# Attention's branch product as seven Strassen products, with its quadrant sums and the pooling's moving sums accumulated in DRAM

## The chip, the cores and the metric

The kernel runs on one core of one Trainium2 chip. The metric is the device time in microseconds of one execution; the median of three is given. A profile is one further execution, recorded instruction by instruction; its span runs from the first to the last recorded instruction.

## The reference

One decoder block on 1024 tokens of width 1024, all in float32. What matters here is its first half:

```python
h = _rmsnorm(x, g_mix_pre[l])
proj = jnp.einsum('bsd,de->bse', h, w_in[l]) + b_in[l]
u_pool, q, k, v, gates = jnp.split(proj, IN_SPLITS, axis=-1)
y_pool = _multiscale_pool(u_pool, w_pool[l], pool_scale[l])
...
y_attn = _sliding_window_sink_attention(...)
g = jax.nn.sigmoid(gates.astype(jnp.float32)).astype(x.dtype)
g_pool, g_attn = g[..., :D_MODEL], g[..., D_MODEL:]
merged = (g_pool * jnp.einsum('bsc,cd->bsd', y_pool, w_branch_pool[l])
          + g_attn * jnp.einsum('bsc,cd->bsd', y_attn, w_branch_attn[l]))
mix = jnp.einsum('bsd,de->bse', merged, w_out[l])
```

`_multiscale_pool` takes 512 channels in four groups of 128, and for each group subtracts the value itself from the mean over the last 2, 4, 8 or 16 tokens (fewer at the start). The attention has 8 query heads of 64, so the attention branch multiplies a 1024 x 512 by a 512 x 1024 matrix. After `mix` come a norm, a squared-ReLU MLP of width 4096 and another norm.

## The kernel before

Every matmul is float32 in three passes (`PASSES`): each operand is split into a rounded part `hi` (ScalarE, L101) and the rest `lo` (VectorE, L104), and hi x hi, hi x lo and lo x hi are added in PSUM. A matmul has 128 x 128 weights and 512 columns. Data is stored with features on the partitions and tokens along the free dimension.

The stages follow each other: q, k and v; attention, in whose gaps the pool projections `u` are made (`u_half`, stored to `u_dram`) and whose outputs are stored and accumulated in `y_dram`; the gates; the attention branch; the pool branch; the output product; the MLP.

The gates, a 1024 x 1024 by 1024 x 2048 product, are already seven Strassen products per pair p of column blocks (`Pairs`, p from 0 to 7): products 1 and 2 of all pairs first, then `rest(p)` with products 6, 7, 5, 4, 3, of 12 matmuls each. Operand sums are made by VectorE (L484 to L494), results close with a scale (L713, L717), a sigmoid on ScalarE and a store to `z_dram`.

The attention branch is `branch(w_ba[m], ...)` for m from 0 to 7: load the weights, split them, and multiply 4 k-tiles in three passes for both halves `th` of the tokens (`mm_fm`, L445 and L447) into two banks, which VectorE multiplies into the gate tiles `zg` (L932). Its right side is read by `load_attn` from `y_dram` during the last gate pair: four quadrants, each [128, 2, 512], split once. Between column blocks, `pool_part` loads a group's `u` and computes its pooled difference on VectorE (`pool_in`): log2(w) additions of a shifted copy (L692), each with a small copy of the edge (L693), then scale and subtract; a split follows. The pool branch then does the same as the attention branch with weights `wbp_dram` and right side `ysp`.

`wo_load` and `wo_add` make sums of quadrants of the output weights: SP loads a quadrant into SBUF, and a GpSimd transfer with `accum_op` adds the other (L966).

Order of work: in most of the first half the program order of PE, VectorE and ScalarE is written by hand (`manual_schedule`); in the gates' second pass and the branches a scheduler of the tile framework places each engine's instructions, SP's and GpSimd's included. Tiles come from pools with a fixed number of buffers: a load waits until the last reader of its buffer is done. DMA completions are counted on eight semaphores for SP and ScalarE together and eight for GpSimd, in turn, so that a transfer also waits for the one that used its semaphore before. SP, ScalarE and GpSimd start their instructions in order, so a wait holds up all that stands behind it.

## Time and profile before

| | |
|---|---|
| time, median of 3 (lowest to highest) | 1110.14 us (1108.49 to 1111.05) |
| the profiled execution | 1109.43 us |
| its span | 1107.6 us |
| instructions | 13855 |
| mean granted TensorE clock | 0.998 |
| DMA: moved, mean rate | 203.71 MB, 184 GB/s |

The profile page gives busy time per engine, slices of the span, the chain of work that ended last and the costliest groups. PE is TensorE's matmul stream, PEld its weight loads, DVE VectorE, ACT ScalarE, POOL GpSimd, SP the engine that issues most DMAs. A row such as `PE mm L445 <- ACT wh L101: 0.2, 1, 0.2` reads: PE's instruction of line 445 writing tile mm waited for ScalarE's of line 101 writing wh, 0.2 us in total, once, 0.2 us at the longest. In the timeline the columns are start, duration, engine, line, operation and tiles, and in brackets the idle time before it with who ended it.

### The profile page before, as it was taken

The page shows a single profiled execution, that of the slowest core. Times are in us where ns is not written, and L with a number is a line of the kernel's source. Part 1 is how long each engine was busy: PE and PEld are TensorE (multiplying, and loading weights), DVE is VectorE, ACT ScalarE, POOL GpSimd, SP SyncE. Part 2 cuts the span into 40 slices and gives each one's busy share as a digit, 9 for nine tenths or more (in the row PEclk, how much of TensorE's full clock was granted, in tenths as well). Part 3 has the DMA queues.
Part 4 walks back from the last instruction along what each step waited for, and adds up shares of the span by engine and source line. Part 5 has one row for each costly group of instructions (what it writes and reads, how often), then busy time and mean ns, then how long its engine had stood idle before and what let it go on. Part 6 is the DMA issues. An engine that isn't in the chain of part 4 may idle for free.

```text
span 1107.6 us, 13855 instructions
## 1 busy us (share of the span) xinstructions
PE 1097.7 (99%) x5108; PEld 907.5 (82%) x5108; DVE 807.1 (73%) x1175; ACT 547.6 (49%) x916; POOL 62.7 (6%) x107
## 2 busy tenths in 40 slices
PE   9999999999999999999999999999999999999997
PEld 7888788888888888878888888888888888888886
DVE  5578867899768796899878867666548944456596
ACT  7466656444432337587555654444434434344342
POOL 0344220000001120000000000000000000000000
PEclk9999999999999999999999999999999999999999
DMA  9406578355677581570457645445597535534673
GB/s 349 161 11 137 149 169 278 132 191 209 224 256 246 152 186 58 192 271 32 162 197 264 242 169 199 146 151 199 178 371 232 189 98 174 177 102 152 204 229 119
DMA packets 89747, 203.71 MB, mean 184 GB/s; under 512 B 8400, under 2 KB 21072, under 8 KB 89680
## 3 DMA queue, kind: packets, MB, share of 16 engines
q1 hardware_dynamic: 77536, 176.88, 48.0%
q10 hardware_dynamic: 5616, 19.66, 4.6%
q0 software_dynamic: 6528, 6.29, 4.0%
q8 instruction: 40, 0.66, 0.3%
q14 instruction: 27, 0.22, 0.1%
HBM read 147.23 MB, written 55.58 MB: 183 GB/s over the span
## 4 chain that ended last, share of the span: by engine, by line
PE 88%; DVE 5%; DMA 3%; ACT 2%; issue 2%; DVEq 0%; SPq 0%; ACTq 0%
PE mm L511 24%; PE at L511 16%; PE at L1406 16%; PE mm L1406 12%; PE mm L601 4%; PE mm L187 3%; PE mm L445 2%; PE at L196 1%; PE at L419 1%; PE mm L447 1%; PE sc L355 1%; PE sc L187 1%; DMA d<-spill_dram 1%; PE at L1048 1%; PE mm L1048 1%
## 5 line engine op out<-in xcount | busy, mean ns | idle before, releaser
L1406 PE MATMUL at<-ar,wh 128*128 128x512 f32 x744 | 169.6, 389 | 0.0
L1406 PEld LDWEIGHTS at<-ar,wh 128*128 128x128 f32 x744 | 139.6, 188 | 29.3 <-DVE ar L104 0.4
L104 DVE TENSOR_TENSOR wh<-raw,wh 128x1024 fp32r<-128x1024 f32 x53 | 64.8, 1223 | 99.4 <-ACT wh L101 99.4
L1406 PE MATMUL mm<-ar,wh 128*128 128x512 f32 x576 | 131.0, 389 | 0.0
L101 ACT CAST wh<-raw 128x1024 fp32r<-128x1024 f32 x53 | 55.8, 1053 | 146.7 <-PE at L1406 71.6
L1406 PEld LDWEIGHTS mm<-ar,wh 128*128 128x128 f32 x576 | 108.1, 188 | 22.4
L101 ACT CAST wh<-st 128x512 fp32r<-128x512 f32 (+1 forms) x97 | 61.6, 646 | 74.4 <-PE at L511 19.9
L104 DVE TENSOR_TENSOR wh<-st,wh 128x512 fp32r<-128x512 f32 (+1 forms) x97 | 68.8, 719 | 27.8 <-ACT wh L101 25.3
L511 PE MATMUL mm<-gr,wh 128*128 128x512 f32 x333 | 80.4, 391 | 0.0
L511 PEld LDWEIGHTS mm<-gr,wh 128*128 128x128 f32 x333 | 62.1, 188 | 13.1 <-DVE gr L1087 0.4
L511 PE MATMUL mm<-T,wx 128*128 128x512 f32 x288 | 67.6, 389 | 0.0
L511 PEld LDWEIGHTS mm<-T,wx 128*128 128x128 f32 x288 | 54.1, 188 | 11.2
L511 PE MATMUL at<-T,wx 128*128 128x512 f32 x252 | 59.1, 389 | 0.0
L511 PEld LDWEIGHTS at<-T,wx 128*128 128x128 f32 x252 | 47.3, 188 | 9.8
L511 PE MATMUL mm<-x,wh 128*128 128x512 f32 x240 | 55.2, 389 | 0.0
L511 PEld LDWEIGHTS mm<-x,wh 128*128 128x128 f32 x240 | 45.0, 188 | 9.4
L104 DVE TENSOR_TENSOR ar<-B,ar 128x1024 fp32r<-128x1024 f32 x37 | 45.1, 1219 | 4.0 <-ACT ar L101 3.9
L601 PE MATMUL mm<-x,wh 128*128 128x512 f32 x192 | 47.5, 395 | 0.0
L101 ACT CAST ar<-B 128x1024 fp32r<-128x1024 f32 x37 | 38.9, 1051 | 5.9 <-DMA B<-in_w_dn_dram 3.0
L601 PEld LDWEIGHTS mm<-x,wh 128*128 128x128 f32 x192 | 35.3, 188 | 7.7
L511 PE MATMUL at<-gr,wh 128*128 128x512 f32 x150 | 36.7, 390 | 0.0
L101 ACT CAST wx<-ws 128x512 fp32r<-128x512 f32 x30 | 18.6, 620 | 32.7 <-DVE ws L487 17.9
(384 smaller groups left out, 2162.4 us busy)
## 6 DMA issues: line engine op xcount, KB each, us to landing
raw<-f_dram SPq DMA_DIRECT2D x53, 512.0 KB, 3.7
f_dram<-g SPq DMA_DIRECT2D x30, 512.0 KB, 3.3
B<-in_w_dn_dram SPq DMA_DIRECT2D x24, 512.0 KB, 6.3
st<-in_w_up_dram SPq DMA_DIRECT2D x20, 512.0 KB, 4.1
st<-in_w_g_dram SPq DMA_DIRECT2D x18, 512.0 KB, 4.6
f_dram<-g ACTq DMA_DIRECT2D x17, 512.0 KB, 2.6
g<-spill_dram SPq DMA_DIRECT2D x16, 512.0 KB, 5.4
raw<-in_w_dn_dram SPq DMA_DIRECT2D x16, 512.0 KB, 4.7
```

The lines of the kernel that those rows point to most:

```text
L101: act.copy(hi, src)
L104: eng.tensor_tensor(lo, src, f32(hi), ALU.subtract)
L187: pe.matmul(bq, xs_[k][n // 4][:, xh, n % 4 * P:(n % 4 + 1) * P], wq[k][:, h, :], start=k == 0 and j == 0, stop=k == NK - 1 and j == 2)
L196: pe.matmul(bkv_of(n), xs_[k][n // 4][:, xh, n % 4 * P:(n % 4 + 1) * P], wkv[k // 2][:, h, k % 2, :], start=k == 0 and j == 0 and not (joi ...
L355: pe.matmul(sb[:, kv, i, :nk], qt[r, qx, m * P:(m + 1) * P], kx[r, k0:k0 + nk], start=j == 0, stop=j == 2)
L419: pe.matmul(flat(yb), v[:, kv, :], flat(p[:, 4 * kv:4 * kv + 4]), start=j == 0, stop=j == len(mms) - 1)
L445: pe.matmul(bs[th], whi[:, k, :], rhs(k, hl, th), start=k == 0 and hl == 0, stop=False)
L447: pe.matmul(bs[th], wlo[:, k, :], rhs(k, 0, th), start=False, stop=k == nk - 1)
L511: pe.matmul(b, w[:, wh, kt, :], xo[kt][:, xh, :], start=not after and kt == 0 and j == 0, stop=kt == 3 and j == 2, skip_group_check=after)
L601: pe.matmul(b, (whi, wlo)[h][:, k, :], xr(k, xh, th), start=j == 0, stop=j == len(mms) - 1)
L1048: pe.matmul(bs[t], gop[i][kt // 2][gh][:, kt % 2, t * P:(t + 1) * P], wop[i][kt // 2][wh][:, kt % 2], start=not after and kt == 0 and j == ...
L1406: pe.matmul(bs[t], fo[fh][:, k2, t * P:(t + 1) * P], wo_[wh][:, k2, :], start=not after and s2 == 0 and k2 == 0 and j == 0, stop=s2 == NS ...
```

## The change

The attention branch becomes seven products (`Halves`) on 2 x 2 quadrants: the weights of a pair of column blocks give A11, A12, A21, A22 and the sums S1 to S4, the attention output gives B11, B21, B22 and T1 to T4. For p from 0 to 3, `first(p)` does products 1 and 2, `rest(p)` products 5, 6, 3, 7, 4; each is 2 k-tiles x 3 passes = 6 matmuls of 512 columns. Product 6 is added onto product 1 in its bank, then 7, then 4; 3 is added onto 5. ScalarE copies the bank out after 1, 5 and 1+6, VectorE reads it after 2, 3, 7 and 4, and the next product into that bank comes after the read.

The sums T1 to T4 are made in DRAM (`quad_sums`, in the spill buffer): a quadrant is loaded, negated on ScalarE and stored by GpSimd, and further quadrants are added by accumulating transfers from DRAM to DRAM. T1 and T4 come out negated and are negated again when they are split. The moving sums are made in the same way (`window_sums`): `u` is stored twice, and for each step a GpSimd transfer adds the sum of the step before, shifted by 1, 2, 4 or 8 tokens; from the second step on it first copies it. `pool_in` then needs only a scale on ScalarE, the edge, and one subtraction.

The gates' second pass is written differently too: `side()` after each product makes one operand of the next pair and runs the new steps from a table `extra`, keyed by pair and step; SP's and GpSimd's orders are now as written (`manual_schedule`), and loads come two pairs ahead. The sum of output weights `sums` is loaded in pair 2 and added to in pair 3 of the branch, without the copy that tied it to a gate tile.

```diff
             nc.sync.dma_start(u_dram[gi], u)
+            nc.sync.dma_start(sum_dram[gi][0], u)
...
-        while step < w:
-            t = place()
-            dve.tensor_tensor(t[:, step:], src[:, step:], src[:, :S - step], ALU.add)
-            dve.tensor_copy(t[:, :step], src[:, :step])
-            src, step = t, 2 * step
...
+    def window_sums(step):
+        for gi in (1, 0, 2, 3):
+            if 1 << step < WINDOWS[gi]:
+                src, dst = (sum_dram[gi][step - 1] if step else u_dram[gi]), sum_dram[gi][step]
+                if step:
+                    pool.dma_start(dst, src, max_dma_last_dim=4096)
+                pool.dma_start(dst[:, 1 << step:], src[:, :S - (1 << step)], accum_op=ALU.add)
+    def pool_in(gi, u, t):
+        w, bias = WINDOWS[gi], vec[:, V_BU + gi:V_BU + gi + 1]
+        act.activation(u, u, AF.Identity, bias=bias)
+        edge = t[:, :w - 1]
+        dve.scalar_tensor_tensor(edge, edge, float(w), cst[:, C_CNT:C_CNT + w - 1], ALU.mult, ALU.mult)
+        act.activation(t, t, AF.Identity, bias=bias, scale=1.0 / w)
+        dve.tensor_tensor(u, t, u, ALU.subtract)
...
+    def quad_sums(part):
+        if part == 0:
+            negate(("T1", "T3"), 0, 1)
+            add("T3", y_dram[1][:, 2:4])
+            add("T1", y_dram[0][:, 0:2])
+        else:
+            negate(("T4",), 1, 0)
+            pool.dma_start(t_dram["T2"], t_dram["T3"], max_dma_last_dim=4096)
+            add("T2", y_dram[0][:, 0:2])
+            add("T4", t_dram["T2"])
...
+        PRODUCT = {1: ("A11", "B11"), 2: ("A12", "B21"), 3: ("S4", "B22"), 4: ("A22", "T4"),
+                   5: ("S1", "T1"), 6: ("S2", "T2"), 7: ("S3", "T3")}
...
+        def rest(self, p, sides, between):
+            z, x, t, t2 = zg[self.base, p], self.x.pop(p), self.tmp.pop(p), g32([2, 512])
+            y = self.bank(p)
+            self.mm(y, p, 5)
+            act.copy(t2[:, 0], y)
+            sides[0]()
+            self.mm(x, p, 6, True)
+            act.copy(t[:, 0], x)
+            sides[1]()
+            self.mm(y, p, 3, True)
+            dve.tensor_tensor(t[:, 0], t[:, 0], y, ALU.add)
+            dve.tensor_tensor(z[1][:, 0], z[1][:, 0], t[:, 0], ALU.mult)
+            sides[2]()
+            self.mm(x, p, 7, True)
+            dve.tensor_tensor(t2[:, 0], t2[:, 0], x, ALU.add)
+            dve.tensor_tensor(z[1][:, 1], z[1][:, 1], t2[:, 0], ALU.mult)
+            sides[3]()
+            between()
+            self.mm(x, p, 4, True)
+            dve.tensor_tensor(z[0][:, 1], z[0][:, 1], x, ALU.mult)
...
+        extra = {(0, 2): lambda: quad_sums(0), (1, 0): lambda: quad_sums(1), (1, 3): lambda: window_sums(1),
+                 (2, 3): lambda: window_sums(2), (3, 3): lambda: window_sums(3),
...
+                 (7, 3): lambda: (ba.load("T4"), ba.split("T3", gr))}
...
-    for m in range(8):
-        branch(w_ba[m], lambda k, hl, th: asp[th][k // 2][hl][:, k % 2, :], 8, m)
+        for p in range(4):
...
+            pool_load(p)
+            if p == 2:
+                sums = wo_load((1, 0), a32)
+            elif p == 3:
+                wo_add(sums, (1, 1))
+            ba.rest(p, (nothing if p < 0 else lambda: w_next(p), nothing, lambda: w_split(p),
+                        lambda: pool_split(p)),
+                    (lambda: ba.first(p + 2)) if p < 2 else nothing)
```

What this moves, in the order of the built programs. PE at the head of the attention branch, before (yahi and yalo are the split attention output, wh the split weights, mm_491 and mm_492 the banks of the two halves of the tokens):

```order
L445 MATMUL mm_491_3135<-yahi_475_3058,wh_489_3131 128x512
L445 MATMUL mm_491_3135<-yalo_476_3059,wh_489_3131 128x512
L445 MATMUL mm_492_3136<-yahi_478_3064,wh_489_3131 128x512
L445 MATMUL mm_492_3136<-yalo_479_3065,wh_489_3131 128x512
L447 MATMUL mm_491_3135<-yahi_475_3058,wh_490_3132 128x512
L447 MATMUL mm_492_3136<-yahi_478_3064,wh_490_3132 128x512
```

Each of the eight column blocks has four such rows of six, in two banks; neither bank is read before all four k-tiles are in. After, PE from the end of product 5 of pair 0 over its product 6 to its product 7 (at_510 is the bank of products 1, 6, 7 and 4 of pair 0, at_526 that of 5 and 3, at_534 that of product 1 of pair 2; gr and wo are split quadrants of the attention output, ar and wh split weights; a second run through the same three passes is left out):

```order
L983 MATMUL at_526_3266<-wo_496_3122,ar_451_2835 128x512
L983 MATMUL at_510_3207<-gr_504_3163,ar_450_2834 128x512
L983 MATMUL at_510_3207<-gr_505_3164,ar_450_2834 128x512
L983 MATMUL at_510_3207<-gr_504_3163,ar_451_2835 128x512
L983 MATMUL at_534_3318<-wo_470_2982,wh_528_3279 128x512
L983 MATMUL at_534_3318<-wo_471_2983,wh_528_3279 128x512
L983 MATMUL at_534_3318<-wo_470_2982,wh_529_3280 128x512
L983 MATMUL at_510_3207<-gr_507_3182,wh_448_2832 128x512
```

The bank at_510 holds product 1 already, so its product 6 stands behind the copy of line 994 out of it, and product 7 behind that of line 1007; between 6 and 7 stand four matmuls of another bank.

ScalarE in the branch after, with the semaphores that each instruction waits for (L994, L1004 and L1007 are the copies after product 1, product 5 and products 1+6; at_510 and mm_515 are the banks of pairs 0 and 1 for 1, 6, 7 and 4, at_526 and mm_542 those for 5 and 3; z_ is the last gate, d_ are the pooling's tiles, ar and wh take split weights):

```order
L994 COPY g_511_3208<-at_510_3207 128x512 [waits PE_49]
L719 DMA spill_dram<-z_472_2986 128x1024 [waits Activation_49]
L994 COPY g_516_3234<-mm_515_3233 128x512 [waits PE_49]
L1007 COPY g_511_3208<-at_510_3207 128x512 [waits DVE_49,PE_49]
L1004 COPY g_525_3265<-at_526_3266 128x512
L994 COPY g_535_3319<-at_534_3318 128x512 [waits PE_49]
L104 CAST ar_546_3367<-ws_543_3360 128x768 [waits DVE_49,PE_49]
L104 CAST wh_544_3365<-st_520_3255 128x1024 [waits DMAHW3_49,PE_49]
L704 ACTIVATE d_523_3261<-d_523_3261,vec_83 128x1024 [waits DMAHW6_49,DMAHW4_49]
L1004 COPY g_541_3351<-mm_542_3352 128x512 [waits DVE_49,PE_49]
L707 ACTIVATE d_524_3262<-d_524_3262,vec_83 128x1024 [waits DMAHW7_49,DVE_49]
L1007 COPY g_516_3234<-mm_515_3233 128x512 [waits PE_49,Activation_49]
```

Before, the same stretch of ScalarE held the last sigmoids, casts of weights, one bias per pooling group and the cast of its difference, and nothing that reads PSUM. Now the copies of pair 1 (L1004, L1007) stand behind two casts and the pooling's L704 and L707, of 768 and 1024 elements.

GpSimd after, from the first store of a negated quadrant to the first window sums (all names are pieces of the spill buffer in DRAM except neg, a negated quadrant in SBUF, and y_dram; DMASW are GpSimd's DMA semaphores):

```order
L859 DMA spill_dram<-neg_396_2403 128x1024 [waits DMASW4_49,Activation_49]
L859 DMA spill_dram<-neg_396_2403 128x1024 [waits DMASW5_49]
L862 DMA spill_dram<-y_dram 128x1024 [waits DMASW5_49,DMASW6_49,DMASW2_49,DMASW7_49,DMASW1_49,DMASW0_49]
L862 DMA spill_dram<-y_dram 128x1024 [waits DMASW4_49]
L859 DMA spill_dram<-neg_407_2476 128x1024 [waits Activation_49]
L871 DMA spill_dram<-spill_dram 128x1024 [waits DMASW6_49]
L862 DMA spill_dram<-y_dram 128x1024 [waits DMASW1_49]
L862 DMA spill_dram<-spill_dram 128x1024 [waits DMASW3_49,DMASW2_49,DMASW0_49]
L698 DMA spill_dram<-spill_dram 128x1024
L699 DMA spill_dram<-spill_dram 128x1022 [waits DMASW4_49]
L698 DMA spill_dram<-spill_dram 128x1024
L699 DMA spill_dram<-spill_dram 128x1022 [waits DMASW7_49,DMASW6_49]
```

Eight more rows of L698 and L699 follow, the last an addition of 1016 columns, and then the sums of the output weights (L1066). Before, these sums (L966) came next after the additions into y_dram; now twenty transfers stand ahead of them, and most of these wait for the landing of one just before.

214 lines of the change are left out of this document (156 added, 58 removed).

## The prediction

> **What bounds the kernel now.** I read the page first, its busy line and its chain of waits.
>
> ```profile
> span 1107.6 us, 13855 instructions
> PE 1097.7 (99%) x5108; PEld 907.5 (82%) x5108; DVE 807.1 (73%) x1175; ACT 547.6 (49%) x916; POOL 62.7 (6%) x107
> PE 88%; DVE 5%; DMA 3%; ACT 2%; issue 2%; DVEq 0%; SPq 0%; ACTq 0%
> ```
>
> TensorE is busy throughout and the chain that ends last is 88% TensorE. A busy PE need not be at its peak, so I next asked who PE waited for. These are all of its waits in the run:
>
> ```profile
> PE mm L205 <- DVE zeros L183: 1.5, 1, 1.5
> PE sc L355 <- DVE s L364: 0.8, 2, 0.5
> PE at L1094 <- DVE x L1063: 0.4, 1, 0.4
> PE mm L445 <- ACT wh L101: 0.2, 1, 0.2
> ```
>
> Under 3 us of 1107.6. Then the stages around the change, by windows (columns: PE, PEld, DVE, ACT, POOL busy; granted clock; DMA share; GB/s): the second pass over the gates, the attention branch, the pool branch, the start of the output product.
>
> ```profile
> 209.70:318.90 109.20, 109.17 (x482) 89.94 (x481) 91.49 (x137) 49.17 (x67) 0.00 (x0) 1.00 0.62 210
> 318.90:362.40 43.50, 43.50 (x193) 36.03 (x192) 35.19 (x57) 12.63 (x15) 4.16 (x4) 1.00 0.79 251
> 362.40:406.00 43.60, 43.45 (x192) 35.55 (x191) 37.09 (x44) 15.12 (x18) 10.06 (x9) 1.00 0.67 173
> 406.00:440.00 34.00, 34.00 (x152) 28.15 (x151) 23.92 (x23) 20.12 (x27) 1.91 (x2) 1.00 0.35 84
> ```
>
> PE has no hole in any of them and the granted clock is 1.00. So a matmul taken away here shortens the run by its own pitch, unless a new wait appears. VectorE is the next busiest (84% in the gates, 81% in the attention branch); ScalarE has half its time free.
>
> **The saving.** The attention branch has 8 column blocks x 4 k-tiles x 3 passes x 2 halves = 192 matmuls. After: 4 pairs x 7 products x 2 k-tiles x 3 passes = 168. The rows of the order (3223 to 3199) show the same 24 fewer and nothing else taken from PE. Their pitch, from the first matmul of the branch and the first of the next one (PE's timeline):
>
> ```profile
> 318.89 0.39 PE L445 MATMUL mm<-yahi,wh 128*128 128x512 f32 x1
> ...
> 362.41 0.39 PE L445 MATMUL mm<-yphi,wh 128*128 128x512 f32 x1
> ```
>
> 43.52 / 192 = 0.2267 us each, weight load hidden. 24 x 0.2267 = 5.44 us. The Trainium skill (TensorE: Matmul & The Clock Gate, section "Wait — 56ns, not 53.3ns?") gives 512 columns at 2.4 GHz plus about 2.5 ns, 215.7 ns; by that the saving would be 5.18 us. The row decides.
>
> **What the new chain on PSUM may give back.** In each pair, products 1, 6, 7 and 4 accumulate in one bank and 5 and 3 in another, so products 3, 7 and 4 cannot start before ScalarE or VectorE has read the bank. Each read is covered by one other product, 6 x 0.2267 = 1.36 us. What such a read takes, from ScalarE's timeline and PE's at the output product, where blocks of 12 matmuls are copied out:
>
> ```profile
> 406.41 11.04 PE L1048 MATMUL at<-wo,gr 128*128 128x512 f32 x48
> ```
>
> ```profile
> 409.33 0.59 ACT L1185 COPY x<-at 128x512 f32<-128x512 f32 x1 [5.96 <-PE at L1048]
> 412.05 0.59 ACT L1185 COPY x<-at 128x512 f32<-128x512 f32 x1 [2.13 <-PE at L1048]
> ...
> 416.13 1.06 ACT L101 CAST gr<-g 128x1024 fp32r<-128x1024 f32 x1 [0.77 <-PE at L1048]
> ```
>
> The first block of 12 is handed over at 406.41 + 2.72 = 409.13; the copy starts 0.20 later and takes 0.59. With 0.20 back to PE (an estimate: the same lag) it is 0.99 of the 1.36: free, with 0.37 to spare, if ScalarE is idle. It is not always: by the order the copies of pairs 1 to 3 mostly stand behind a 1024-wide operation of the pooling, and these take 1.05 to 1.15:
>
> ```profile
> 318.35 1.15 ACT L709 ACTIVATE z<-z,vec 128x1024 f32<-128x1024 f32 x1 [1.36 <-DVE z L717]
> ```
>
> A copy that meets one just begun is 1.15 - 0.37 = 0.78 late. Eight such copies (M5 and M1+M6 of four pairs): between 0 and 8 x 0.78 = 6.2 us. ScalarE's load in the stage is 12 copies x 0.59, 12 pooling operations x 1.1, and about 5 us of weights and last sigmoids: 25 of 38 us, and most long operations can run while PE is inside an earlier product, so I take 0.7 us.
>
> VectorE's pace, from its timeline (start, duration; successive starts give the cost):
>
> ```profile
> 398.97 1.22 DVE L104 TENSOR_TENSOR ar<-g,ar 128x1024 fp32r<-128x1024 f32 x1
> 400.11 1.22 DVE L1187 SCALAR_TENSOR_TENSOR g<-g,g 128x1024 f32<-128x1024 f32 x1
> 401.24 1.28 DVE L932 TENSOR_TENSOR g<-g,mm 128x512 f32<-128x512 f32 x2
> 402.44 1.23 DVE L104 TENSOR_TENSOR gr<-g,gr 128x1024 fp32r<-128x1024 f32 x1
> ```
>
> So 1.14 us for 1024 elements, 0.60 for 512, and by the slope 0.33 for 256 and 0.87 for 768. Attention branch after: 28 reads and products x 0.60, one pair's weight sums 4 x 0.33, splits of weights 1.14 + 1.14 + 0.87, pooling 4 x (0.15 + 1.14 + 1.14), the last gate scales and one pool weight 1.8: about 33 of 38 us (87%). It drops the ten moving-sum additions and their edge copies. The last two gate pairs are the tight place. Each has 13.6 us of PE. Pair 6: 4.74 (five bank reads, two scales) + 5.4 (pair 7's operands) + 2.28 (two quadrant splits) + 2.0 (weights 0) = 14.4. Pair 7: 4.74 + 4.56 (four quadrants) + 1.3 + 2.0 + 1.3 (weights) = 13.9. That is 28.3 against 27.2: VectorE enters the branch 1.1 us late. What it is late with are the last gate's scales, on which the last sigmoid and then ScalarE's first branch copy wait: 318.89 + 0.2 + 1.1 + 0.6 + 0.6 + 1.15 + 0.59 = 323.1, and product 6 of pair 0, which needs that copy, stands at 318.89 + 30 x 0.2267 = 325.7. Covered by 2.6 us; if the cover went, each microsecond would be one of PE's. I charge nothing.
>
> **The accumulating transfers.** GpSimd has nothing in this stage before (0.00 in the first window row); after, it has 20 transfers in one queue, each of which waits for an earlier one to land. What the trace has for them are plain stores, and accumulations into SBUF (issue rows; median us to landing), and GpSimd's own time to issue:
>
> ```profile
> s<-in_w_o_dram POOLq DMA_DIRECT2D x8, 512.0 KB, 7.3
> y_dram<-yt POOLq DMA_DIRECT2D x16, 128.0 KB, 5.2
> st<-y_dram SPq DMA_DIRECT2D x4, 512.0 KB, 4.8
> d<-spill_dram SPq DMA_DIRECT2D x4, 512.0 KB, 4.2
> ```
>
> ```profile
> 384.77 2.44 POOL L966 DMA_DIRECT2D s<-in_w_o_dram  x2 [2.15 <-DVE wo L104]
> ```
>
> Neither shows a 512 KB accumulation into DRAM, so I bound it by 5.2 (the accumulation that lands in DRAM, a quarter the size) and by the slowest pair, in the window from 350 to 360 us, where the DMA engines were nearly full in its second half (busy tenths in 40 slices):
>
> ```profile
> DMA  0000000072589997688989679799899994999999
> ...
> s<-in_w_o_dram POOLq DMA_DIRECT2D x2, 512.0 KB, 8.6
> ```
>
> The chain starts when the first quadrant is loaded and negated. Its load stands behind the gate loads that SP issued here:
>
> ```profile
> 216.53 1.13 SPq L475 DMA_DIRECT2D st<-in_w_g_dram  x2
> ```
>
> 217.7 + 4.8 + 1.15 = 223.7. By the waits in the order 12 landings follow each other (the second negated store, T3's sum, the copy to T2, T2's sum; then five copies, of which each but the first is issued behind an addition; the last additions for window 8 and, by copy and addition, window 16), with six issues of 1.22 (2.44 / 2) between: 223.7 + 7.3 + 12 x L = 231 + 12 x L. L = 5.2 gives 293, 7.3 gives 319, 8.6 gives 334. The last sum (window 16) is loaded by SP just ahead of the pool branch's first weights, which must be issued by about 350 (the pool branch begins at 318.89 + 162 x 0.2267 = 355.6, and load, cast and subtraction take some 5). I take 8.6, since the added traffic (20 x 0.5 MB in a stage whose engines were busy 0.62) fills the engines too: 16 us to spare, cost nothing. T1, T2 and T4 land by 231 + 4 x 8.6 = 265 and are loaded from 290 on. Break-even is L = (350 - 231) / 12 = 9.9.
>
> The Trainium skill has a rule that speaks against this (SBUF — State Buffer, section "SBUF: two separate sides"): while VectorE runs in a two-port mode GpSimd cannot write descriptors, and a transfer of 620 ns took 3100. By that each landing would be 2.5 us later, 8.6 + 2.5 = 11.1, the chain would end at 364 and PE would wait some 14 us. The trace does not bear it out: the row at 384.77 shows 1.22 us per issue in a stage where VectorE is busy 37.09 of 43.6.
>
> The other moves cost nothing that I can find: four more stores of u on SP (0.33 us to issue each, in the attention stage, where PE waited only for the masks), four accumulations that GpSimd does ahead of stores that are read 50 us later, and SP's written-out order, in which the loads of T4 and of weights 2 wait for the last gate pair's first product (318.89 - 57 x 0.2267 = 306.0) and are used from 318.89 + 36 x 0.2267 = 327 on. The sums of the out weights, two loads on SP and two accumulations on GpSimd, move from behind column block 4 to pairs 2 and 3; they stand behind the chain, which ends before their old place:
>
> ```profile
> 355.42 1.24 POOL L966 DMA_DIRECT2D s<-in_w_o_dram  x1 [3.22 <-DMA s<-in_w_o_dram]
> ```
>
> **The sum.** The profiled execution took 1109.43 us, 1.8 outside its span, 0.7 below the median of the three runs, 1110.14. 1109.43 - 5.44 + 0.7 = 1104.7; against the median 1105.4.
>
> **Rivals.** First, the bank chain eats the gain: ScalarE's copies come late at most of the eight places, 8 x 0.5 = 4.0 us. Then 1110.14 - 5.44 + 4.0 = 1108.7, no change that can be told (0.2%, 2.2 us, is about what a measurement of this kernel can tell). For it: the in-order ScalarE queue and a slack of only 0.37. Against: 13 us of the stage's ScalarE time are free. Second, on the slower side: the chain on GpSimd runs late. From L = 9.9 on, SP stands at the window-16 sum with the pool branch's weights behind it, and each further microsecond of L is 12 of PE's. It makes the run slower by over 0.2% from a wait of 7.7 us, L = 10.6. At L = 11 the chain ends at 363: 1105.4 + 13 = 1118. For it: no row shows a DRAM to DRAM accumulation, with rows that begin one to eight elements off. Against: both rows of accumulations lie below 9. The skill's port rule would give this case too (1119). That the change does not do what it says is excluded by the 24 fewer matmul rows.
>
> **How the numbers follow.** Forecast 0.68: 1105.4, from 1103.2 (no wait at all is 1104.7, less the 1.6 by which single runs lie below the median) to 1107.5. Bank chain 0.17, around 1108.7, to 1110.4. Late transfers 0.15, 1112 and up. Range 1103.2 to 1110.4, leaving out the last case and little else. Faster 0.68 + 0.05 = 0.73; same 0.10 + 0.01 = 0.11; slower 0.02 + 0.14 = 0.16.
>
> **What would show it.** Right: 24 fewer matmuls on PE (168 in the branch), the branch 38.1 to 39 us long, PE's list of waits with at most 1 us from the branch's lines on ScalarE or VectorE, and the last accumulation landed before 340. Wrong: waits of PE on the branch's copies that sum to 3 us or more; a PE hole at the start of the pool branch, with SP waiting for a DMA on the spill buffer; landings of the new transfers above 9.9 us; or VectorE backlog that shows as PE waits inside the last gate pairs.

## The result, and the profile after

| | before | after |
|---|---|---|
| time, median (lowest to highest, runs) | 1109.85 us (1108.49 to 1111.05, 4) | 1123.12 us (1122.15 to 1127.06, 4) |
| ratio, 95% interval | | 1.0127 (1.0100 to 1.0154) |
| the profiled execution, its span | 1109.43, 1107.6 us | 1127.06, 1125.3 us |

The change makes the kernel 13.3 us slower; forecast was 4.7 us faster, with a range of 1103.2 to 1110.4 us. The profiled execution of after is the slowest of its four, so its stages show 17.7 us of loss in the span and not 13.

From the page of after, its span, busy line and the shares of the chain that ended last:

```profile
span 1125.3 us, 13878 instructions
...
PE 1102.1 (98%) x5084; PEld 906.5 (81%) x5084; DVE 814.5 (72%) x1182; ACT 564.3 (50%) x937; POOL 77.9 (7%) x129
...
PE 79%; DMA 10%; DVE 6%; ACT 3%; issue 2%; SPq 0%; DVEq 0%; ACTq 0%
```

PE has 24 instructions fewer, as announced, but 4.4 us more busy time, and the chain that ended last goes over transfers for 10% of the span instead of 3%.

To place the loss I cut both traces at the first matmul of the second pass over the gates, at that of the attention branch and at that of the output product. Columns as in the prediction: length, then PE, PEld, DVE, ACT and POOL busy, granted clock, DMA share, GB/s. Before:

```profile
223.69:318.89 95.20, 95.20 (x421) 78.84 (x420) 78.23 (x115) 41.21 (x54) 0.00 (x0) 1.00 0.65 219
318.89:406.41 87.52, 87.37 (x386) 71.92 (x384) 72.69 (x101) 27.77 (x33) 14.63 (x14) 1.00 0.73 212
```

After:

```profile
225.05:335.23 110.18, 101.47 (x421) 81.52 (x420) 87.27 (x131) 48.50 (x62) 13.78 (x20) 0.96 0.93 296
335.23:422.44 87.21, 84.33 (x362) 68.50 (x360) 70.58 (x92) 38.46 (x47) 12.89 (x12) 0.98 0.82 246
```

The second pass over the gates, whose 420 matmuls the change does not touch, takes 110.18 us instead of 95.20: 14.98 of the 17.7 us. Its DMA share went from 0.65 to 0.93. The two branches, where the 24 matmuls are gone, are only 0.31 shorter instead of 5.44. The rest is small: the pass starts 1.36 later, and what follows the branches takes 1.7 longer (1125.3 - 422.44 = 702.9 against 1107.6 - 406.41 = 701.2).

PE's waits of after, the first four of the list:

```profile
PE at L514 <- DVE z L543: 2.9, 2, 2.0
PE mm L514 <- DVE z L546: 2.9, 2, 2.4
PE mm L448 <- ACT wh L104: 2.9, 1, 2.9
PE at L514 <- ACT ar L104: 2.4, 1, 2.4
```

L514 is the gates' matmul, L448 the pool branch's. None of the four is in the attention branch (L983): the new chain on PSUM banks, which the prediction feared, makes PE wait nowhere. In the gates it is VectorE's reads of the banks (L543, L546) and one cast that come late. With one more hole of 0.5 (a further row of the list) the six holes of that pass sum to 8.7 us.

Why VectorE is late, from its own waits in that window:

```profile
DVE ws L963 <- DMA st<-in_w_ba_dram: 7.3, 2, 4.6
DVE ws L487 <- DMA g<-in_w_g_dram: 4.0, 1, 4.0
```

It stands for loads, of gate weights (L487) and of the branch's weights (L963), 11.3 us together, and as its order is fixed the bank reads stand behind them. One hole in full, from the chain of waits (start, length, what):

```profile
234.73 0.33 SPq L478
...
235.11 9.64 DMA g<-in_w_g_dram
...
244.77 0.69 DVE ws L487
...
246.03 0.68 DVE g L535
...
248.68 0.63 ACT ar L104
...
249.39 7.34 PE at L514 x24
```

A weight load issued at 234.73 takes 9.64 us to land. VectorE makes an operand sum of it, the sum is split, and PE starts 2.42 us late. The loads of the branch's weights stand in the same way ahead of the holes that end at 280.47 and 331.13.

How the same kind of load lands, from the transfers issued between 225 and 320 us (median us to landing in the last column), before and after:

```profile
st<-in_w_g_dram SPq DMA_DIRECT2D x5, 512.0 KB, 3.5
```

```profile
q0 software_dynamic: 2448, 8.91, 39.3%
...
st<-in_w_g_dram SPq DMA_DIRECT2D x6, 512.0 KB, 7.7
```

The kernel before has no row of GpSimd's queue (q0) in this window. Now this queue takes 39.3% of the sixteen engines' time, and the gate loads land in 7.7 us instead of 3.5.

The holes cost more than their length. The first 6 us after the one at 249.39, in steps of 2 us:

```profile
249.39:251.39 2.00, 2.00 (x7) 1.64 (x8) 2.00 (x4) 1.48 (x3) 0.00 (x0) 0.79 1.01 309
251.39:253.39 2.00, 2.00 (x6) 1.51 (x6) 1.46 (x3) 0.00 (x0) 0.00 (x0) 0.50 0.94 322
253.39:255.39 2.00, 2.00 (x9) 1.62 (x8) 1.50 (x3) 0.12 (x1) 0.85 (x1) 0.86 0.78 180
```

PE is busy throughout, but the granted clock falls to 0.50. The 24 matmuls from 249.39 on last until 256.56: 7.17 us instead of 24 x 0.2267 = 5.44, so 1.7 us on top of the hole of 2.42. 110.18 - 95.20 - 8.7 leaves 6.3 us. After two more of the holes (1.99 and 2.42 us) the next 24 matmuls last 7.22 and 7.16, of which the last 12 lie already in the branch: the three stretches make up 4.9 us of the 6.3 (1.7, 1.8 and, up to the end of the pass, 1.4).

In the branches the loss stands at one place, the start of the pool branch. SP's timeline there (start, duration), then ScalarE's:

```profile
361.82 3.22 SPq L1044 DMA_DIRECT2D d<-spill_dram  x2
365.09 0.42 SPq L438 DMA_DIRECT2D st<-wbp_dram  x1
...
371.14 0.33 SPq L438 DMA_DIRECT2D st<-wbp_dram  x1
```

```profile
381.92 0.62 ACT L104 CAST wh<-st 128x512 fp32r<-128x512 f32 x1 [6.48 <-DMA st<-wbp_dram]
```

The weights `wbp` stand on SP behind the loads of the last pooling group, which wait for buffers of the group before (SP's waits name `DVE d L708`, 8.5 us in two); the second one leaves at 371.14, its cast starts 10.8 us later, and PE stands 2.88 us for it, with 1.8 us lost on slow matmuls behind it.

The chain on GpSimd itself ran at about the pace that was forecast. Its last addition, and how the DRAM to DRAM transfers landed (from the timeline and the transfers between 215 and 385 us):

```profile
334.41 0.81 POOL L699 DMA_DIRECT2D spill_dram<-spill_dram  x1 [5.96 <-DMA spill_dram<-spill_dram]
```

```profile
spill_dram<-spill_dram POOLq DMA_DIRECT2D x8, 512.0 KB, 8.8
```

The row above has the copies and the additions of full quadrants. The last addition, of 1016 columns, lands 8.3 us after its issue, at 342.7.

### The profile page after: what moved, and what is told of

The parts are those of the page before. It is cut to its first block, busy times and chain, and to the rows that moved or that the text cites. A ratio compares the mean times of both kernels' runs of the same rounds, so it can differ in the third digit from the quotient of the medians.

```text
span 1125.3 us, 13878 instructions
## 1 busy us (share of the span) xinstructions
PE 1102.1 (98%) x5084; PEld 906.5 (81%) x5084; DVE 814.5 (72%) x1182; ACT 564.3 (50%) x937; POOL 77.9 (7%) x129
## 4 chain that ended last, share of the span: by engine, by line
PE 79%; DMA 10%; DVE 6%; ACT 3%; issue 2%; SPq 0%; DVEq 0%; ACTq 0%
PE mm L514 17%; PE at L1582 15%; PE at L514 13%; PE mm L1582 12%; PE mm L607 4%; PE mm L190 3%; PE mm L448 2%; DMA q<-spill_dram 2%; DMA st<-in_w_ba_dram 2%; DMA st<-wbp_dram 1%; DMA g<-in_w_g_dram 1%; PE at L199 1%; PE at L983 1%; PE at L422 1%; DMA st<-in_w_g_dram 1%
## 5 line engine op out<-in xcount | busy, mean ns | idle before, releaser
L514 PE MATMUL mm<-gr,wh 128*128 128x512 f32 x333 | 80.5, 391 | 0.9 <-DVE gr L1263 0.6
L514 PEld LDWEIGHTS mm<-gr,wh 128*128 128x128 f32 x333 | 62.0, 188 | 14.4 <-DVE gr L1263 1.3
L514 PE MATMUL mm<-T,wx 128*128 128x512 f32 x288 | 67.5, 389 | 0.0
L514 PEld LDWEIGHTS mm<-T,wx 128*128 128x128 f32 x288 | 54.1, 188 | 11.2
L514 PE MATMUL mm<-x,wh 128*128 128x512 f32 x240 | 57.3, 397 | 3.1 <-DVE z L546 2.9
L514 PE MATMUL at<-T,wx 128*128 128x512 f32 x252 | 59.1, 389 | 0.0
L514 PEld LDWEIGHTS mm<-x,wh 128*128 128x128 f32 x240 | 45.5, 191 | 14.1 <-issue 2.8
L514 PEld LDWEIGHTS at<-T,wx 128*128 128x128 f32 x252 | 47.3, 188 | 9.8
L514 PE MATMUL at<-T,wh 128*128 128x512 f32 x138 | 35.0, 394 | 5.3 <-DVE z L543 2.9
L514 PE MATMUL at<-gr,wh 128*128 128x512 f32 x150 | 39.7, 414 | 0.0
```

Of the source, the lines that this page charges most:

```text
L514: pe.matmul(b, w[:, wh, kt, :], xo[kt][:, xh, :], start=not after and kt == 0 and j == 0, stop=kt == 3 and j == 2, skip_group_check=after)
```

## The experiments

Theory A: the bytes of the twenty transfers fill the sixteen DMA engines, loads land late, and engines that take their work in order pass that on to PE. Theory B: the newly written order (the table `extra`, SP's order by hand) makes the loads late, whatever GpSimd moves. Unless said otherwise the diffs are against the changed kernel; times are medians with lowest to highest, and ratios stand against the kernel before on the same chip, with 95% intervals. A line of three dots marks where a diff is cut.

**1. The traffic taken away.** 17 of the 20 transfers move 64 of 1024 columns; the tensors that they made are filled by plain stores in the attention stage.

```diff
-        pool.dma_start(t_dram[name], src, accum_op=ALU.add, max_dma_last_dim=4096)
+        pool.dma_start(t_dram[name][:, :, :32], src[:, :, :32], accum_op=ALU.add, max_dma_last_dim=4096)
...
+                end = 64 if step else S - 1
-                pool.dma_start(dst[:, 1 << step:], src[:, :S - (1 << step)], accum_op=ALU.add)
+                pool.dma_start(dst[:, 1 << step:end + (1 << step)], src[:, :end], accum_op=ALU.add)
```

> The changed kernel with 17 of the accumulating and copying transfers cut to 64 of 1024 columns (the sums are left out in the other columns, where an earlier store of u or of a negated quadrant remains, so the output is not the block's; seven plain stores are added in the attention stage for that). Same instructions, same order, same waits, a sixteenth of the bytes. Theory A (the bytes: the transfers fill the DMA engines, loads for the gate pairs and for the branch land late, VectorE stands in its queue at what needs them, bank reads come late, TensorE stops and then runs at a lower clock): the gates' second pass goes back from 110.2 us to 95-97, the time to 1104-1108. Theory B (the written order of SP and the table of steps put loads and VectorE's work at the wrong places, whatever the transfers move): the pass stays near 110 us and the time above 1118.

1110.97 us (1108.66 to 1112.95, 10 runs); 1.0010 (0.9999 to 1.0021). The second pass takes 96.19 us with the order of the changed kernel, at a granted clock of 1.00, and the gate loads land in 4.4 us: Theory B falls for that stage. The time is above the 1104 to 1108 expected: the hole at the pool branch stays (3.17 us), and the pass begins at 226.88 us, 1.8 later than in the changed kernel. The added stores stand ahead of it; that they are the reason was not tried apart.

**2. The traffic alone, in the kernel before.** Twenty DRAM to DRAM transfers of 512 KB from `z_dram` in a chain, ten copies and ten shifted additions, whose results nobody reads; started at the second gate pair. The second kernel has copies in place of the additions. Diff against the kernel before:

```diff
...
+    def traffic():
+        src = [z_dram[0], z_dram[1]]
+        for i in range(5):
+            dst = [extra_dram[2 * i], extra_dram[2 * i + 1]]
+            for d, s_ in zip(dst, src):
+                pool.dma_start(d, s_, max_dma_last_dim=4096)
+            for d, s_ in zip(dst, src):
+                pool.dma_start(d[:, 2:], s_[:, :S - 2], accum_op=ALU.add)
+            src = dst
...
+        if p == 1:
+            traffic()
```

> The kernel before, with 20 transfers of 512 KB from DRAM to DRAM added on GpSimd (10 copies, 10 additions shifted by 2 columns, two chains side by side, started by the first gates' store; nobody reads them). Theory A: slower by 5 to 15 us, with VectorE waiting for gate loads and TensorE for VectorE in the gates' second pass, although the order of the loads is the old one. Theory B: no change beyond 2 us.

> As the kernel before with 20 added transfers (1134.98), but all 20 are plain copies, none accumulates. If it is the bytes, an addition reads its target as well, and 20 copies cost two thirds: 8 us in a DMA load nearer to that of before, 1114 to 1122. If any DRAM to DRAM transfer costs the same, 1133 to 1136. If an accumulation alone does the harm, under 1112.

With additions 1134.98 us (1134.66 to 1135.45), 1.0225 (1.0210 to 1.0240); with copies alone 1123.55 (1123.25 to 1125.62), 1.0128 (1.0113 to 1.0143). The second pass with additions, then with copies:

```profile
224.41:344.89 120.48, 103.54 (x421) 83.70 (x420) 77.94 (x116) 41.12 (x54) 13.76 (x20) 0.92 0.85 260
```

```profile
223.96:334.87 110.91, 100.38 (x422) 81.42 (x420) 77.90 (x115) 41.06 (x54) 10.61 (x20) 0.95 0.81 282
```

Transfers whose results nothing reads cost the kernel before 25.3 and 15.7 us in this stage, the additions more than the 5 to 15 us expected. So the traffic alone suffices, without the new order. That both cost more than in the changed kernel fits its loads being issued two pairs ahead, which was not tried apart. GpSimd's queue in the 95 us from 225 on, with additions and with copies (packets, MB, share of the sixteen engines):

```profile
q0 software_dynamic: 2880, 10.48, 45.8%
```

```profile
q0 software_dynamic: 2240, 10.48, 32.3%
```

A copied megabyte takes 32.3 / 10.48 = 3.1% of that time, an accumulated one (45.8 - 16.15) / 5.24 = 5.7%, about 1.8 times as much (under load, so both hold some waiting).

**3. The pool branch's weights first.** SP loads the first two `wbp` weights ahead of the last pooling group.

```diff
+    ahead = {}
+    def pool_weights(m):
+        ahead[m] = stage([4, P])
+        nc.sync.dma_start(ahead[m], wbp_dram[m])
...
+            if p == 3:
+                pool_weights(0)
+                pool_weights(1)
```

> The changed kernel with one edit: SP loads the first two column blocks' weights of the pool branch ahead of the last group's u and sum instead of behind them. If the wait of 2.9 us at the pool branch and the slow matmuls behind it (some 2 us) come from SP's order: 1118 to 1119.5. If they come from the transfers alone (the load took 10.8 us to land, but no added transfer is under way by then): no change, 1122 to 1124.

1118.73 us (1117.76 to 1119.61); 1.0080 (1.0065 to 1.0095), 4.4 us below the changed kernel's median. In SP's timeline both weights now leave at 357.26, and PE's list of waits has no row of L448 any more. The second pass stays long (108.13 us).

**4. Both together.** The weights first and narrow transfers as in 1, but without the added stores: product 6 and the pooling read tensors that stand there already, so the sums are left out of the result.

```diff
+                end = 64 if step else S - 1
...
-            nc.sync.dma_start(self.raw[name], self.quad(*q) if q else t_dram[name])
+            nc.sync.dma_start(self.raw[name], self.quad(*q) if q else t_dram["T3" if name == "T2" else name])
...
+                pool_weights(0)
+                pool_weights(1)
```

> The changed kernel with the weights first and 17 of the transfers cut to 64 columns, without the stores that the first such run added: T2 and the moving sums are read from other places of the same size (T3, and the u that is stored twice), so they are left out of what is computed. This is the product of seven alone, without the traffic. Theory A and the order of the weights: nothing but the 24 matmuls and the chain of banks is left, 1109.7 - 5.4 = 1104.3, up to 1106. If the sums in the first such run were slow for another reason than its stores and the weights: 1107 to 1110.

1106.25 us (1104.50 to 1107.30, 6 runs); 0.9966 (0.9952 to 0.9979): faster than before by 3.8 us. Its two windows:

```profile
225.72:320.95 95.23, 95.23 (x422) 78.86 (x420) 86.60 (x131) 48.48 (x61) 14.73 (x20) 1.00 0.76 259
320.95:403.36 82.41, 82.36 (x362) 67.13 (x361) 70.36 (x93) 38.87 (x47) 12.52 (x11) 1.00 0.82 252
```

The second pass is back at 95.23 us although VectorE, ScalarE and the count of transfers are those of the changed kernel, and the branches take 82.41, 5.11 less than before. Gate loads land in 4.3 us:

```profile
st<-in_w_g_dram SPq DMA_DIRECT2D x6, 512.0 KB, 4.3
```

**5. The sums made elsewhere.** Three kernels take sums off the DMA engines, to see whether another engine has room: the moving sums on VectorE as before (T1 to T4 still in DRAM); the moving sums on GpSimd; and T1 to T4 on GpSimd as well, with nothing left from DRAM to DRAM. The core of the second and the third:

```diff
-                pool.dma_start(dst[:, 1 << step:], src[:, :S - (1 << step)], accum_op=ALU.add)
+            pool.tensor_tensor(t[:, step:], src[:, step:], src[:, :S - step], ALU.add)
+            act.copy(t[:, :step], src[:, :step])
...
+                pool.tensor_tensor(r["T1"], r["B11"], r["B12"], ALU.subtract)
+                pool.tensor_tensor(r["T3"], r["B22"], r["B12"], ALU.subtract)
```

> The changed kernel with the pooling's moving sums on VectorE in SBUF as before the change, the quadrant sums still in DRAM: 8 of the 20 transfers stay. Theory A: the gates' second pass loses 3 to 7 us of the 15, but VectorE has some 47 us of work in the 38 us of the branch (33 + 10 x 1.14 + edges), so the branch grows by up to 9: 1110 to 1118. Theory B: the pass still loses 15 and the branch 9: about 1130.

> As the one with the sums on VectorE, but the ten additions are GpSimd's in SBUF and the edge copies ScalarE's; 8 of the 20 transfers stay. GpSimd took 0.46 us for 128 elements, so 1 to 3.7 us for 1024 and 10 to 37 us in all. Theory A: the gates' second pass loses 3 to 7 us, the branch keeps its 38 if GpSimd's additions are in time: 1106 to 1112. Theory B: the pass loses 15: 1120.

> No transfer from DRAM to DRAM is left: T1 to T4 are made by four GpSimd subtractions and additions in SBUF from the four quadrants (12 of 16 buffers of x are free by then), and the moving sums by ten GpSimd additions in the branch, as in the run with the sums on GpSimd (1.9 to 2.5 us each there). Theory A: the gates' second pass goes from 104.4 us there to 95-97; the branch keeps that run's losses (waits of 3.7, 1.5 and 2.6 us): 1112 to 1118. Theory B (VectorE is too full in the last pairs, whatever the traffic): the pass stays above 100 us.

1125.65 us (1125.0 to 1126.4), 1.0141 (1.0126 to 1.0156); 1126.04 (1123.04 to 1127.33), 1.0135 (1.0113 to 1.0157); 1124.58 (1122.1 to 1125.37), 1.0129 (1.0114 to 1.0144). None is better than the changed kernel, and none comes to what theory A let expect (1106 to 1118). The second pass gets shorter with the traffic (102.49, 104.38 and 100.57 us), but the branches pay: PE waits 9.0 and 2.0 us for VectorE in the first, 3.7 for ScalarE and 2.6 and 1.5 for VectorE in the second, 3.5 and 1.7 for VectorE in the third. In the third the pass is still 5.4 us longer than before, with no transfer from DRAM to DRAM left; experiment 6 shows a reason.

**6. GpSimd in the second pass.** The moving sums by GpSimd during gate pairs 0 to 2 and stored, T1 to T4 on GpSimd, weights first.

```diff
+    def moving(gi):
+        src, step = xq32(), 1
+        nc.sync.dma_start(src, u_dram[gi])
+        while step < WINDOWS[gi]:
+            t = xq32()
+            pool.tensor_tensor(t[:, step:], src[:, step:], src[:, :S - step], ALU.add)
+            pool.tensor_copy(t[:, :step], src[:, :step])
+            src, step = t, 2 * step
+        pool.dma_start(sum_dram[gi], src)
```

> As before this with the moving sums made by GpSimd during gate pairs 0 to 2 in free buffers of x and stored (four plain stores), so that the branch is that of the changed kernel; the weight sums of pair 0 are asked for 3 products later, and the first two weights of the pool branch are loaded ahead of the last group of the pooling. Theory A with the second loss (SP's order at the pool branch): all of the 24 matmuls' 5.44 us is left over: 1104 to 1107, gates' second pass 95-97, pool branch without a wait over 1 us. If GpSimd's additions slow VectorE where they run side by side, the pass is longer by up to 5: 1109 to 1112.

1127.90 us (1123.27 to 1129.55); 1.0157 (1.0128 to 1.0185), where 1104 to 1112 was expected. Here theory A alone fails: the second pass is long at a DMA share of only 0.60.

```profile
224.60:336.74 112.14, 102.04 (x422) 81.65 (x420) 107.62 (x131) 46.38 (x59) 41.99 (x28) 0.95 0.60 215
```

VectorE has the same 131 instructions but is busy 107.6 us of 112.1. GpSimd's timeline, then VectorE's:

```profile
247.06 2.23 POOL L1097 TENSOR_TENSOR q<-q 128x1022 f32<-128x1022 f32 x1
```

```profile
247.46 0.68 DVE L535 TENSOR_TENSOR g<-g,at 128x512 f32<-128x512 f32 x1
248.06 1.78 DVE L490 TENSOR_TENSOR ws<-ws,st 128x512 f32<-128x512 f32 x1
```

The first VectorE operation reads a PSUM bank (`at`) and takes its 0.68 us. The second has both inputs in SBUF, lasts 1.78 us and ends at 249.84, 0.55 after GpSimd's addition (249.29). A second mechanism, then, with the same end: VectorE late at the banks. In this pass no wait of VectorE names a load.

**7. The sums moved earlier.** Four kernels move the traffic out of the second pass, all with the weights first. The chain of T1 to T4 in the first pass over the gates and the moving sums begun in the attention stage; the same, with each group's last moving sum added into SBUF on loading; the quadrant sums and all moving sums begun in the second half of the first pass; and that with only the first quadrant sums and the first moving sums early, with the branch's first weight sums three products later.

```diff
+            if p == 2:
+                neg_load(0, 1)
+            elif p == 4:
+                quad_sums(0)
+            elif p == 6:
+                neg_load(1, 0)
+            elif p == 7:
+                quad_sums(1)
+                window_sums(2)
+                window_sums(3)
...
+        pool.dma_start(dif[gi][1][:, h:], src[:, :S - h], accum_op=ALU.add)
```

> The run with the weights first (1118.73), and the added transfers start earlier: the moving sums behind each group's u in the attention stage, the quadrant sums in the gates' first pass, in the same number and size. GpSimd's queue was idle there for 49 us in the changed kernel, and DMA was at 0.4 in the last slice of the first pass. Theory A: the traffic is spread over the attention stage and the first pass, the gates' second pass goes from 108 us to 96-100 and the time to 1104-1110, unless GpSimd's waits for landings hold up the value casts of the attention, or loads in the attention stage, which would show as waits there. If the place of the traffic doesn't matter, because the stages ahead are as full: 1116 to 1120.

> As with the chain started early, and the last step of each moving sum is accumulated into SBUF on its way into the branch: 6 transfers fewer in DRAM, 4 accumulations into SBUF in the branch. Theory A: 0 to 3 us below the run with the chain started early, unless the accumulation comes too late for a pair of the branch (a load of 5 us and one of 8 stand ahead of the pooling of that pair, whose place is 8 us behind): then waits of ScalarE's copies show in the branch, and it is slower by up to 8.

> The run with the weights first (1118.73), with the same 20 transfers started in the second half of the gates' first pass, where DMA was busy 0.39 and 0.49 of the time, and without anything of SP standing behind the end of the attention (that made the first pass lose 23 us in the run with the chain started early). Theory A, with the place of the traffic: the part that fits into 195 to 225 us comes out of the second pass, which goes from 108 us to 98-104, and the time to 1106-1114; the first pass keeps its 58 us. If the DMA engines are full for the whole of the chain whatever its start, the second pass stays at 106 or more.

> As the run with the weight sums later, and the first four quadrant transfers start some 14 us earlier, in the gates' first pass, before pair 1's loads; the moving sums stay behind them. If the loss depends on which load a transfer runs beside: pair 1's wait (2.0 us for ScalarE behind a gate load of 9.6 us) goes too, 1110 to 1114. If only the sum of the bytes counts: as the run with the weight sums later.

1131.38 us (1128.24 to 1137.88, 5 runs), 1.0192 (1.0175 to 1.0209); 1124.02 (1119.08 to 1128.16), 1.0127 (1.0093 to 1.0162); 1123.31 (1120.57 to 1124.17), 1.0117 (1.0100 to 1.0134); 1123.48 (1118.71 to 1124.4), 1.0117 (1.0094 to 1.0139). None comes to the 1104 to 1114 us expected if the place of the traffic counted. The second kernel's second pass is as good as before's:

```profile
234.51:329.71 95.20, 95.20 (x421) 78.85 (x420) 87.57 (x132) 46.08 (x59) 2.23 (x3) 1.00 0.74 247
```

but it starts at 234.51, after a hole of 8.0 us in the first pass. In the first kernel SP stood 20.5 us at once for `y_dram`, with the gate loads behind it:

```profile
SPq L858 <- DMA y_dram<-yt: 21.2, 2, 20.5
```

and PE waited 22.6 us for casts of gate weights. So in these two the loss lies ahead of the second pass, and the chains of waits lead there to additions into `y_dram` that GpSimd issues behind the new transfers; whether the bytes or that order made them late was not separated. In the third and fourth the second pass is still long, 110.82 and 104.87 us: in the third the weight sums (L978) made VectorE stand 14.1 us at once, one PE hole of 11.5, and in the fourth PE waits 7.3 us ahead of the pass and 6.5 in it. No place that was tried is free.

**8. The weight sums alone later.** As 3, with `ba.weights(0)` moved from (4, 2) to (5, 0) in `extra`.

```diff
-                 (4, 2): lambda: w_todo.append(ba.weights(0)),
+                 (5, 0): lambda: w_todo.append(ba.weights(0)),
```

> The run with the weights first (1118.73), in which VectorE stood 4.6 us at the weight sums of pair 0 for their load and TensorE then 2 us (and some 2 us of slow matmuls), with one edit: these weight sums stand three products later in VectorE's order. If the loss comes through the places at which VectorE waits for a load: that wait is gone and the time is 3 to 5 us lower, 1114 to 1116. If the lateness only moves to the next load: 1117 to 1119.

1117.52 us (1113.33 to 1119.0); 1.0062 (1.0038 to 1.0087), and the interval overlaps that of experiment 3. The second pass takes 109.68 us. VectorE still stood for loads of that kind, 10.1 us in two waits, since the first of these sums had moved only two rows down its built order. The question, whether a later place for the sums spares the hole, stays open.

**9. Fewer bytes, and VectorE as it was.** Moving sums on VectorE, the eight quadrant transfers in the first pass, weights first; then also the last group's `u` in a buffer of its own, loaded in pair 1.

```diff
+            t = place()
+            dve.tensor_tensor(t[:, step:], src[:, step:], src[:, :S - step], ALU.add)
+            dve.tensor_copy(t[:, :step], src[:, :step])
...
+        last[3] = flat(bcp.tile([P, 2, 512], F32, tag="bc", name=nm("d3")))
+        nc.sync.dma_start(last[3], u_dram[3])
```

> Three findings put together: the pooling's moving sums on VectorE as before the change (8 of the 20 transfers stay), the quadrant sums started in the gates' first pass, and the first weights of the pool branch loaded ahead of the last group. In the run that started them in the first pass with the last step loaded, the gates' second pass had its 95.2 us beside 5 such transfers at a DMA share of 0.74. If the loss comes from the DMA share alone: a second pass of 95-98 instead of 102.5, VectorE's 47 us of work in the branch cost 3 to 9 us as in the first run of that kind, 1107 to 1113. If each load that comes late finds another wait: 1116 or more.

> As the run before it (1118.85), whose one large loss left was a wait of 10.6 us near the end of the branch: the last group's u was issued at 355.4, when a buffer came free, landed 8.7 us later, and VectorE's bank reads stand among that group's additions. Its u now has a buffer of its own (the one that the negated quadrants have left) and is loaded in pair 1. If that load was the cause: the wait shrinks to what VectorE's own work asks for, 2 to 4 us, and the time is 1107 to 1111. If VectorE is simply too full: less than 4 us better, above 1114.

1118.85 us (1118.55 to 1119.28), 1.0087 (1.0070 to 1.0104); 1116.04 (1114.65 to 1117.66), 1.0058 (1.0042 to 1.0075). In both the second pass is nearly whole (96.69 us at share 0.72 in the first). What is left is one hole in the branch, in the first:

```profile
370.26 2.92 PE L993 MATMUL mm<-wo,wh 128*128 128x512 f32 x6 [10.59 <-DVE g L1024]
```

The first kernel misses the 1107 to 1113 expected. In the second the hole is 8.65 us, and around it VectorE is full, 18.09 of 19 us:

```profile
357.00:376.00 19.00, 10.22 (x34) 7.57 (x33) 18.09 (x29) 4.37 (x5) 0.00 (x0) 0.73 0.70 229
```

That speaks for the moving sums having to leave VectorE once seven products bring their bank reads and operand splits to it; the rows show VectorE full and do not separate what fills it. No kernel that computes the whole block beat the kernel before.

All kernels side by side: the second pass over the gates, its DMA share, the median landing of its loads `st<-in_w_g_dram`, and its length.

| kernel | share | landing, us | length, us |
|---|---|---|---|
| 5, third | 0.60 | 3.7 | 100.57 |
| 6 | 0.60 | 5.0 | 112.14 |
| before | 0.65 | 3.5 | 95.20 |
| 7, first | 0.70 | 5.4 | 98.98 |
| 9, first | 0.72 | 4.6 | 96.69 |
| 9, second | 0.72 | 4.8 | 96.89 |
| 7, second | 0.74 | 5.2 | 95.20 |
| 4 | 0.76 | 4.3 | 95.23 |
| 1 | 0.78 | 4.4 | 96.19 |
| 5, second | 0.78 | 8.0 | 104.38 |
| 5, first | 0.80 | 7.9 | 102.49 |
| 2, copies | 0.81 | 6.6 | 110.91 |
| 2, additions | 0.85 | 8.4 | 120.48 |
| 7, fourth | 0.88 | 5.0 | 104.87 |
| 7, third | 0.90 | 6.7 | 110.82 |
| after | 0.93 | 7.7 | 110.18 |
| 3 | 0.93 | 7.4 | 108.13 |
| 8 | 0.94 | 8.1 | 109.68 |

From a share of 0.80 on every pass is 7 us or more longer than before, but below it the share does not decide: 0.78 stands beside 96.19 and 104.38 us. The landing of the gate loads tells these two apart (4.4 and 8.0 us), and in every kernel where it is 6.6 us or more the pass is 7 us or more longer. Three lie outside that too: the third of 5 and 6, where GpSimd adds during the pass (in the second of 5 it adds only later, in the branch), and the fourth of 7, where VectorE stood for other transfers (9.8 us for the branch's weights, 8.0 for a store of gates). Share and landing are averages that the holes themselves change; they order the cases and are no thresholds.

## Why the prediction was wrong

**Right: the saving.** 24 matmuls fewer, and with the traffic gone the branches are 5.11 us shorter (experiment 4) against 5.44 forecast.

**Right, and cheaper than charged: the bank chain.** 0.7 us was charged; no row of PE's waits names L994, L1004 or L1007, and the 5.11 of experiment 4 leaves at most 0.33 for it. The first rival (4.0 us from late copies) did not occur.

**Nearly right: the accumulating chain's own pace.** 8.6 us per landing was taken, 8.8 is the median of the full quadrants. The chain was to land at 334 and landed at 342.7, past the 340 named as a sign of being right: it began 2.9 us later (226.58), and by the prediction's own formula 342.7 is 231 + 12 x 9.3. The second rival's point of decision, 9.9, was not reached, and SP asked for the last sum only at 361.82. So the rival's price of 13 us is near the loss by chance and had nothing to do with it. The same holds for the port rule that the prediction cites beside it (the Trainium skill, SBUF — State Buffer, section "SBUF: two separate sides"): the trace shows no sign of it, as the last addition took 0.81 us to issue and 8.3 to land, not 11.1, and VectorE was 79% busy in the stage (87.27 of 110.18).

**Wrong: the step from full engines to no cost.** The failed step reads: "I take 8.6, since the added traffic (20 x 0.5 MB in a stage whose engines were busy 0.62) fills the engines too: 16 us to spare, cost nothing". It drew from the full engines only that the chain itself would be slow, and compared that with the chain's own deadline. But the sixteen engines carry the loads of gate and branch weights too, which are due within microseconds. The gate loads landed in 7.7 us instead of 3.5, VectorE stood 11.3 us for loads, and the second pass over the gates, which the sum did not have as a term, grew by 15.0 us. Experiments 1 and 4 (traffic away, loss away) and 2 (traffic alone, loss there) show it; that VectorE's fixed order carries it to PE is read from the chain of waits and was not separated by a run.

**Wrong: the pool branch's first weights.** The prediction saw SP's order at this place and made the landing of the window sums the danger. They had landed by 342.7. What held SP were the buffers of the pooling group before. It cost 4.4 us (experiment 3).

**Not in the sum: what a hole costs behind itself.** A term "wait of x us" was taken as x. Here a hole of 2.42 cost 4.15.

Together: 1106.25 in experiment 4, within 1 us of the forecast 1105.4, is the case in which both misses are taken away. Its result leaves sums out, so it shows where the loss lay and not a kernel to use. Not explained are about 3 us of the profiled execution, 1.36 ahead of the second pass (it starts between 223.5 and 225.7 us in the runs that put nothing ahead of it) and 1.7 behind the branches.

## What to carry to other kernels

A transfer that nobody waits for still has a price: add its bytes to the DMA share of the stage it lies in, and ask which loads there have only a few microseconds to spare and which in-order engine stands for them. The share alone does not tell: 0.78 cost 1 us in one kernel here and 9 in another. Price accumulation from DRAM to DRAM above a copy of the same size (1.8 times here). Before a chain of work is moved to an idle engine or queue, name what it shares with the busy ones: here the sixteen DMA engines, and for GpSimd VectorE's second SBUF input.

## What the runs showed of the hardware

An accumulating DRAM to DRAM transfer took about 1.8 times the time of the DMA engines that a copy of the same bytes took (experiment 2, under load).

A GpSimd addition of 1022 elements (2.23 us) held a VectorE operation with two SBUF inputs that came during it until it had ended (1.78 us instead of 0.68), and left one with a PSUM input alone (experiment 6). The Trainium skill (SBUF — State Buffer, section "Who interferes with whom") says that a VectorE instruction with two SBUF inputs contends with a GpSimd instruction that reads SBUF; the trace agrees.

The granted clock fell to 0.50 after each of the PE holes of 1.99 to 2.88 us in the changed kernel, for 3.4 us; after one of 2.15 us, in experiment 3, it stayed at 1.00:

```profile
314.00:316.00 2.00, 2.00 (x10) 1.64 (x10) 1.97 (x4) 0.00 (x0) 0.00 (x0) 1.00 1.00 387
```

Where a hole lies decides. By windows of 0.2 us, the four slow stretches of the changed kernel begin at 250.54, 281.26, 332.46 and 383.66 us: the last three are 9, 24 and 39 steps of 3.413 us after the first. In experiment 3 they begin at 249.99 and 280.71; the same steps then have a border at 311.43, in the middle of the hole of 2.15 us (310.41 to 312.56). The traces of the other kernels agree, for holes of 0.9 us and more between 165 and 420 us: with the borders set by a kernel's first slow stretch, a step at full clock in which PE stood 1.99 us or more in such holes was always followed by a slow one, a step with 1.80 us or less never, and between 1.82 and 1.89 us four of five were.

The Trainium skill (TensorE: Matmul & The Clock Gate, section "What's actually happening") has the clock go to half after at least one idle window of about 3.4 us, in windows that run free. The steps above agree with windows that run free; but here a window in which PE stood for little more than half was enough.
